# Sixteen tiles of U of layer 1 split into high and low parts beside the mixers, and the layer change's squares summed on TensorE alone

## The chip, the cores and the metric

The kernel runs on one core of a Trainium2 chip. The metric is the device time of one execution in microseconds (us). TensorE (PE) does the matmuls and loads their weights (PEld), VectorE (DVE) and ScalarE (ACT) work element by element, GpSimd (POOL) can do the same, SyncE (SP) issues most of the DMAs, and POOL issues some.

## The reference

A two-layer diffusion backbone over 256 latent and 256 context tokens of width 1024, all in float32:

```python
for l in range(DEPTH):                                  # DEPTH = 2
    n = modulate(rmsnorm(h, norm1_g[l]), shift, scale)
    p = split(n @ w_in[l])                              # inputs of four mixers and the gates
    ys = [neighborhood_attention, hyena, gqa, diff_attention]   # each on its part of p
    h = h + mod * merge_branches(ys, gates, w_branch[l], w_out[l])
    m = modulate(rmsnorm(h, norm2_g[l]), shift, scale)
    h = h + mod * peer(m, peer_wq[l], peer_keys[l], peer_u[l], peer_v[l])
    # layer 1: latent tokens alone
return rmsnorm(h_lat, final_g)

def peer(x, wq, keys, u_tab, v_tab):    # 16384 experts, 8 heads, top 16 of each
    q = x @ wq;  s = q . keys           # two lists of 128 scores for each head
    best, eidx = top16 of the sums of the two top-16 lists
    g = softmax(best)
    return sum over the chosen experts e: g[e] * gelu(u_tab[e] . x) * v_tab[e]
```

## The kernel before

**Products in float32.** A weight tile `r` (128x1024 float32, 512 KB) is split into a high part `wh` (a rounded copy, made by ACT) and a low part `wl = r - wh` (a subtract on DVE or POOL). `mm3` makes each product of three matmuls (L405 to L407: hi with hi, lo with hi, hi with lo). The raw tiles, the high parts and the low parts each rotate through three buffers (`wraw`, `wh`, `wl`), and all users of weights share these nine.

**Units.** The projections, the gates, the output projection and the query projection come as a list of units (`unit_order`) in each layer: six of neighbourhood attention (`na`), four of `gqa`, six of differential attention (`dif`), 32 gates with six of Hyena (`hyn`) ahead of the ninth, then `out` and `wq`. `Units.load` issues a unit's DMA on SP (L313), `Units.split` makes its two parts (L336 on ACT, L337 on DVE or POOL), `Units.next` splits one or two units ahead and loads up to three ahead. An entry `pre` in this list is a tile of U: it is loaded and split in the same way, and its low part is stored to DRAM by SP (L339, `ulo`). In layer 0 there are 20 of them among the mixers' units; in layer 1 there are none.

**PEER.** Instead of fetching the chosen experts, the kernel computes all 128 tiles of U against the tokens (`u_next`: `load_u` on SP, `split_u` at L1247 and L1248, `u_mm` into `po`, Gelu into a `ga` buffer), scatters the gates g into a dense table of 128x128 per token (`scatter`: one-hot rows `ohA`, `ohB`, `ohC` on DVE and ACT, matmuls at L1560, copies `gblk` at L1562, stores to `gd`), and then multiplies the gated activations with the 128 tiles of V (L1698). The search for the best experts is `lists` (MAX8, MATCH_REPLACE8, FIND_INDEX8 at L1383 to L1387) and `select` (L1442 to L1488), on DVE. U tiles are woven between these as work for PE. For a tile that was a `pre`, `load_u` fetches the low part from DRAM by a DMA on POOL's queue (L1244) and no subtract is made. In layer 1 (256 tokens, so a U tile is 24 matmuls of 128x256) the first 15 low parts are made by POOL and those after them by DVE.

**The change of layers.** After the last tiles of V, the sums are transposed on PE (L401), added to the state `hT` on DVE (L1801), and the next layer's norm is begun: `Rms` squares each 128x256 piece on ACT (L456), adds the squares in pairs on DVE (L462), and sums over the partitions by a matmul with ones (L463); `rstd_of` (L411 to L415) gives the factor, and `norm_apply` (L484 to L486) the normed `nh` and `nl`. At this place alone the squares lie in quarters of tiles of the `wl` and `wh` rings (`Rms(..., "wl")` for tokens 256 to 511, `Rms(0, 256, ew, "wh")` for tokens 0 to 255); other norms use small buffers of their own.

The order of the instructions on each engine is that in which a scheduler put them when the kernel was built; within an engine they start in that order.

Of the kernel before, what the change touches and what calls it, by code (L numbers as in the profile page):

```python
# [8 lines left out]
F32 = mybir.dt.float32  # L9
# [10 lines left out]
P = 128  # L20
D = 1024
KD = 8
T = 512
EPS = 1e-6
DEPTH = 2
# [38 lines left out]

N_PRE = (20, 0)


def unit_order():  # L70

    o = []
    for l in range(DEPTH):
        pre = iter(range(N_PRE[l]))
        proj = lambda kind, n: [x for i in range(n) for x in [(l, 'pre', j) for j in ([] if kind == 'na' and i == 0 else
                                                                                       [next(pre, None)]) if j is not None] + [(l, kind, i)]]
        o += proj('na', 6)
        o += proj('gqa', 4)
        o += proj('dif', 6)
        for i in range(32):  # L80
            if i == 8:
                o += proj('hyn', 6)
            o += [(l, 'gate', i)]
            if N_MOD1 + i < (N_MOD2 if l else N_MOD):
                o += [(l, 'modr', N_MOD1 + i)]

        for kind in ('out', 'wq'):
            o += [(l, kind, i) for i in range(8)] * (1 if l else 2)
        o += LATE_MOD[l]
    return o  # L90
# [58 lines left out]
def lay_out(i):  # L149
# [21 lines left out]
    for l in range(DEPTH):  # L171
# [14 lines left out]
        for k, w in parts.items():  # L186
            for m, u in enumerate(w):
# [18 lines left out]
                                 g['diff_lq2'][l], g['diff_lk2'][l]]))  # L206
        HB.append(g['hy_bias'][l][None])
    order = unit_order()
    a['W'] = np.stack([U[k] for k in dict.fromkeys(order) if k[1] != 'pre'])
    a['WB'] = np.stack(WB)  # L210
# [63 lines left out]
def body(ctx, tc, I, out, dbg=None):  # L274
    nc = tc.nc
    pe, act, dve, pool, sp = nc.tensor, nc.scalar, nc.vector, nc.gpsimd, nc.sync
# [5 lines left out]
    dr = ctx.enter_context(tc.tile_pool(name="dr", bufs=1, space=DRAM))  # L282
# [13 lines left out]
    def po_tile():  # L296
        tick[0] ^= 1
        return psp.tile([P, 512], F32, name=f"po{tick[0]}")

    order = unit_order()  # L300
    place = {k: z for z, k in enumerate(k for k in dict.fromkeys(order) if k[1] != 'pre')}
    ulo_d = [[dr.tile([P, D], F32, name=f"ulo{l}_{j}") for j in range(N_PRE[l])] for l in range(DEPTH)]

    class Units:
        def __init__(self):
# [60 lines left out]
    start = stx.enter_context(tc.tile_pool(name="start", bufs=1))  # L366
# [19 lines left out]
    ones = keep.tile([P, P], F32, name="ones")  # L386
# [52 lines left out]
    class Rms:  # L439
# [17 lines left out]

        def sum(self, k):

            if k % 2:  # L460
                a, b = [self.sq.pop(z)[:, :self.n] for z in (k - 1, k)]
                dve.tensor_tensor(a, a, b, op=ALU.add)  # L462
                pe.matmul(self.ps[:, :self.n], ones, a, start=(k == 1), stop=(k == KD - 1))  # L463
# [122 lines left out]
    for l in range(DEPTH):  # L586
        last = l == DEPTH - 1
        q0 = 256 if last else 0
        n = T - q0
# [648 lines left out]
        def load_u(j):  # L1238
            if j < P:
                ur[j] = wp.tile([P, D], F32, name="wraw", bufs=3)  # L1240
                sp.dma_start(ur[j], I['U'][l, j])
                if j < N_PRE[l]:
                    ul[j] = wp.tile([P, D], F32R, name="wl", bufs=3)
                    pool.dma_start(ul[j], ulo_d[l][j])  # L1244

        def halves(h, lo, r, eng=dve):
            act.activation(h, r, AF.Copy)  # L1247
            return eng.tensor_tensor(lo, r, h.bitcast(F32), op=ALU.subtract)  # L1248

        def split_u(j):  # L1250
            if j >= P:
                return
            h = wp.tile([P, D], F32R, name="wh", bufs=3)
            if j < N_PRE[l]:
                lo = ul.pop(j)
                act.activation(h, ur.pop(j), AF.Copy)
            else:
                lo = wp.tile([P, D], F32R, name="wl", bufs=3)
                halves(h, lo, ur.pop(j), lo_eng[0])
            us[j] = (h, lo)  # L1260
# [23 lines left out]
        def u_next():  # L1284
            j = nu[0]
            if j == 0:
                load_u(0)
                load_u(1)
                split_u(0)
            load_u(j + 2)  # L1290
            split_u(j + 1)
            u_mm(j)
            nu[0] += 1
# [558 lines left out]
```

## Time and profile before

| | before |
|---|---|
| runs | 3037.76, 3040.68, 3041.22 us (median 3040.68) |
| profiled execution | 3041.57 us, its span 3039.8 us |
| busy over the span | PE 2935.4 us, DVE 2270.2, ACT 1480.8, POOL 531.3 |
| granted TensorE clock, mean | 0.989 of full speed |
| layer 1: change of layers / mixers / routing with the first U tiles | 1838 to 1880 / 1880 to 2170 / 2200 to 2350 us |

The span starts with the first instruction on the core and ends with the last; 1.77 us of the profiled execution lie outside it. Busy times of engines overlap. PE is busy nearly all the time, so what counts is how long PE stands still at each place and what it stood waiting for, and, where matmuls are queued but start late, how far their spacing is above the densest one.

### The profile page before, as it was taken

Reading aid. Unit: us, or ns where it says so; the run is one execution under the profiler, and the core shown is the slowest. Engines: PE = TensorE matmul, PEld = TensorE weight load, DVE = VectorE, ACT = ScalarE, POOL = GpSimd, SP = SyncE. Lnnn points to the kernel's source line nnn. Section 1 sums busy time; section 2 is a strip of 40 time slices with the busy share of each in tenths; the row PEclk is TensorE's granted clock in tenths of the full one; section 3 lists DMA queues with packets and bytes.
Section 4 is the critical chain, followed back from the end, with each engine's and each line's share of the span. In section 5 each row is a group of like instructions: output and inputs, shape, how many; then the busy total and the mean of one; then the engine's idle time right before and its main releaser. Section 6 shows DMA issues by size and latency. Waiting matters only on the chain.

```text
span 3039.8 us, 47523 instructions
## 1 busy us (share of the span) xinstructions
PE 2935.4 (97%) x17500; PEld 2593.4 (85%) x17500; DVE 2270.2 (75%) x4818; ACT 1480.8 (49%) x2603; POOL 531.3 (17%) x394
## 2 busy tenths in 40 slices
PE   8999999998999999999999998999899999999998
PEld 5877777897889999999999986888898989989986
DVE  5875986799888777777877687788699667555545
ACT  5555422559853333333333335565548754555443
POOL 1001110140023444444444102000160000000000
PEclk9999999999999999999999999999999999999999
DMA  8544344655689998998988764357555699666644
GB/s 309 180 142 139 119 151 142 200 189 195 230 296 344 326 323 305 312 330 315 321 320 314 266 194 138 96 182 226 193 160 202 214 300 316 217 208 208 211 150 146
DMA packets 271673, 693.42 MB, mean 228 GB/s; under 512 B 22440, under 2 KB 115120, under 8 KB 270928
## 3 DMA queue, kind: packets, MB, share of 16 engines
q1 hardware_dynamic: 228096, 534.85, 52.6%
q0 software_dynamic: 43344, 155.54, 14.7%
q8 instruction: 137, 2.24, 0.3%
q14 instruction: 96, 0.79, 0.1%
HBM read 630.53 MB, written 59.77 MB: 227 GB/s over the span
## 4 chain that ended last, share of the span: by engine, by line
PE 73%; DVE 11%; DMA 4%; ACT 2%; issue 2%; POOL 0%; DVEq 0%; ACTq 0%; POOLq 0%; SPq 0%
PE mm L1698 13%; PE at L1698 12%; PE po L405 9%; PE po L407 9%; PE po L406 9%; PE mm L405 5%; PE mm L406 5%; PE mm L407 5%; PE at L1560 3%; DMA vr<-in_V_dram 2%; DMA wraw<-in_W_dram 2%; PE at L401 1%; DVE junk L527 1%; ACT vh L1247 1%; DVE rep L1385 1%
## 5 line engine op out<-in xcount | busy, mean ns | idle before, releaser
L405 PE MATMUL po<-nh,wh 128*128 128x384 f32 (+1 forms) x2048 | 636.7, 311 | 4.9 <-ACT wh L1247 2.2
L407 PE MATMUL po<-nh,wl 128*128 128x384 f32 (+1 forms) x2048 | 633.9, 310 | 3.2 <-DVE wl L1248 2.6
L1247 ACT ACTIVATE wh<-wraw 128x1024 fp32r<-128x1024 f32 x236 | 249.8, 1059 | 363.5 <-PE po L406 324.0
L405 PEld LDWEIGHTS po<-nh,wh 128*128 128x128 f32 x2048 | 389.3, 190 | 14.5 <-ACT wh L1247 2.8
L407 PEld LDWEIGHTS po<-nh,wl 128*128 128x128 f32 x2048 | 388.8, 190 | 4.9 <-DVE wl L1248 3.5
L1248 DVE TENSOR_TENSOR vl<-vr,vh 128x1024 fp32r<-128x1024 f32 x254 | 310.5, 1222 | 108.4 <-ACT vh L1247 108.1
L1247 ACT ACTIVATE vh<-vr 128x1024 fp32r<-128x1024 f32 x254 | 269.7, 1062 | 232.0 <-DMA vr<-in_V_dram 201.9
L405 PE MATMUL mm<-nh,wh 128*128 128x256 f32 (+1 forms) x1056 | 349.2, 333 | 13.6 <-ACT wh L336 4.2
L1248 DVE TENSOR_TENSOR wl<-wraw,wh 128x1024 fp32r<-128x1024 f32 x221 | 269.6, 1221 | 117.8 <-ACT wh L1247 117.7
L407 PE MATMUL mm<-nh,wl 128*128 128x256 f32 (+1 forms) x1056 | 343.3, 326 | 0.4 <-POOL wl L337 0.4
L406 PE MATMUL po<-nl,wh 128*128 128x384 f32 x1024 | 343.7, 336 | 0.0
L336 ACT ACTIVATE wh<-wraw 128x1024 fp32r<-128x1024 f32 x176 | 185.5, 1057 | 293.5 <-PE mm L406 162.4
L406 PE MATMUL mm<-nl,wh 128*128 128x256 f32 (+1 forms) x992 | 325.1, 329 | 0.0
L406 PE MATMUL po<-nh,wh 128*128 128x256 f32 x1024 | 289.8, 283 | 0.0
L1698 PE MATMUL mm<-vl,Wh 128*128 128x512 f32 x635 | 250.3, 394 | 4.3 <-DVE vl L1248 4.0
L1698 PE MATMUL mm<-vh,Wh 128*128 128x512 f32 x635 | 248.4, 391 | 0.9 <-ACT vh L1247 0.8
L1698 PE MATMUL at<-vh,Wl 128*128 128x512 f32 x635 | 248.5, 391 | 0.0
L1698 PE MATMUL at<-vh,Wh 128*128 128x512 f32 x635 | 248.2, 391 | 0.0
L1698 PE MATMUL mm<-vh,Wl 128*128 128x512 f32 x635 | 247.4, 390 | 0.0
L1698 PE MATMUL at<-vl,Wh 128*128 128x512 f32 x635 | 247.0, 389 | 0.0
L405 PEld LDWEIGHTS mm<-nh,wh 128*128 128x128 f32 x1056 | 205.0, 195 | 40.4 <-ACT wh L336 4.6
L1332 DVE SCALAR_TENSOR_TENSOR gacc<-grow,gdot,gacc 128x1024 f32<-128x1024 f32 x127 | 162.9, 1283 | 90.6 <-DMA grow<-in_V_dram,gix 89.6
(369 smaller groups left out, 6288.2 us busy)
## 6 DMA issues: line engine op xcount, KB each, us to landing
wraw<-in_U_dram SPq DMA_DIRECT2D x276, 512.0 KB
vr<-in_V_dram SPq DMA_DIRECT2D x254, 512.0 KB
wraw<-in_W_dram SPq DMA_DIRECT2D x214, 512.0 KB
gd<-gblk SPq DMA_DIRECT2D x80, 512.0 KB
G<-gd SPq DMA_DIRECT2D x32, 768.0 KB
G<-gd SPq DMA_DIRECT2D x32, 512.0 KB
grow<-in_W_dram SPq DMA_DIRECT2D x24, 512.0 KB
ulo<-wl SPq DMA_DIRECT2D x20, 512.0 KB
```

Source lines behind the costliest of these rows:

```text
L336: act.activation(h, r, AF.Copy)
L401: pe.transpose(o, i, ident)
L405: pe.matmul(ps, w[0], x[0], start=first, stop=False)
L406: pe.matmul(ps, w[0], x[1], start=False, stop=False)
L407: pe.matmul(ps, w[1], x[0], start=False, stop=last)
L527: dve.scalar_tensor_tensor(w if s else junk, w, 1.0, crow[s], op0=ALU.mult, op1=ALU.mult, accum_out=mod[:, u, s:s + 1])
L1247: act.activation(h, r, AF.Copy)
L1248: return eng.tensor_tensor(lo, r, h.bitcast(F32), op=ALU.subtract)
L1332: dve.scalar_tensor_tensor(acc, g, dot[:, e:e + 1], acc, op0=ALU.mult, op1=ALU.add)
L1385: dve.match_replace(rep[:, :nn], v[:, 0:8], x, -3e38)
L1560: pe.matmul(ps4[:, :, z], A[:, :, z], C[:, z, :, h], start=h == 1, stop=h == 0)
L1698: pe.matmul(accs[i][h], w[a][:, i * 128:(i + 1) * 128], v[b][:, h * 512:(h + 1) * 512], start=j == 0 and a + b == 0, stop=j == P - 1 and a ...
```

## The change

The table of pre-made tiles becomes a range for each layer: 0 to 19 in layer 0 as before, and 14 to 29 in layer 1, one ahead of each of the four `gqa`, six `dif` and six `hyn` units of layer 1. Second, where an `Rms` keeps its squares in a ring, the pairwise adds are left out and each of the eight squares goes through its own matmul with ones. Lines from 462 on move down by two.

```diff
-N_PRE = (20, 0)
+PRE = (range(20), range(14, 30))
...
-        pre = iter(range(N_PRE[l]))
-        proj = lambda kind, n: [x for i in range(n) for x in [(l, 'pre', j) for j in ([] if kind == 'na' and i == 0 else
+        pre = iter(PRE[l])
+        proj = lambda kind, n: [x for i in range(n) for x in [(l, 'pre', j) for j in ([] if kind == 'na' and (i == 0 or l) else
...
-    ulo_d = [[dr.tile([P, D], F32, name=f"ulo{l}_{j}") for j in range(N_PRE[l])] for l in range(DEPTH)]
+    ulo_d = [[dr.tile([P, D], F32, name=f"ulo{l}_{j}") for j in range(PRE[l].stop)] for l in range(DEPTH)]
...
         def sum(self, k):
 
-            if k % 2:
+            if self.ring is not None:
+                pe.matmul(self.ps[:, :self.n], ones, self.sq.pop(k), start=(k == 0), stop=(k == KD - 1))
+            elif k % 2:
                 a, b = [self.sq.pop(z)[:, :self.n] for z in (k - 1, k)]
                 dve.tensor_tensor(a, a, b, op=ALU.add)
                 pe.matmul(self.ps[:, :self.n], ones, a, start=(k == 1), stop=(k == KD - 1))
...
-                if j < N_PRE[l]:
+                if j in PRE[l]:
                     ul[j] = wp.tile([P, D], F32R, name="wl", bufs=3)
                     pool.dma_start(ul[j], ulo_d[l][j])
...
-            if j < N_PRE[l]:
+            if j in PRE[l]:
                 lo = ul.pop(j)
                 act.activation(h, ur.pop(j), AF.Copy)
```

The change of layers, DVE's order before, from the first residuals (`hT`) to the first normed piece (`n_x`):

```order
L1801 SCALAR_TENSOR_TENSOR hT<-at,mod_113,hT 128x256 x3
L462 TENSOR_TENSOR wl<-wl 128x256
L1801 SCALAR_TENSOR_TENSOR hT<-mm,mod_113,hT 128x128
L462 TENSOR_TENSOR wl<-wl 128x256
L1801 SCALAR_TENSOR_TENSOR hT<-mm,mod_113,hT 128x128 x7
L412 TENSOR_SCALAR n_t<-po_17404 128x256
L462 TENSOR_TENSOR wh<-wh 128x256
L413 TENSOR_TENSOR n_t<-n_t,n_r_17493 128x256
...
L415 SCALAR_TENSOR_TENSOR n_r_17493<-n_t,n_r_17493 128x256
L462 TENSOR_TENSOR wh<-wh 128x256
L484 SCALAR_TENSOR_TENSOR n_x<-hT,coef_116,n_r_17493 128x256 x3
```

The same place on PE now, from the transposes of the sums of V (`at`, `mm`) to the first projection (L405); L461 is the matmul with ones:

```order
L401 MATMUL at<-kc,grow 128x128 x4
L401 MATMUL mm<-kc,grow 128x128 x3
L401 MATMUL at<-kc,grow 128x128 x4
L461 MATMUL po_17434<-wl,ones 128x256 x4
L401 MATMUL at<-kc,grow 128x128 x6
L401 MATMUL mm<-kc,grow 128x128 x2
...
L461 MATMUL po_17434<-wl,ones 128x256 x3
L401 MATMUL mm<-kc,grow 128x128 x2
L461 MATMUL po_17520<-wh,ones 128x256 x7
L649 MATMUL at<-k_17641,k_17639 64x256
L405 MATMUL mm<-nh,wh 128x256 x2
```

The adds of L462 are gone from DVE, sixteen sums stand on PE where eight stood, four of them between the transposes, and seven in one row right ahead of the projection.

SP's order in the mixers of layer 1, where before there was one load after another of units (L313, with L316 for the gates' second weight):

```order
L316 DMA wbraw<-in_WB_dram 128x256 x3
L313 DMA wraw<-in_W_dram 128x1024 x18
L316 DMA wbraw<-in_WB_dram 128x256
```

and now, from the first gqa unit on:

```order
L313 DMA wraw<-in_U_dram 128x1024
L316 DMA wbraw<-in_WB_dram 128x256
L339 DMA ulo_14_103<-wl 128x1024
L313 DMA wraw<-in_W_dram 128x1024
L313 DMA wraw<-in_U_dram 128x1024
L339 DMA ulo_15_104<-wl 128x1024
L313 DMA wraw<-in_W_dram 128x1024
```

Each store of a low part stands ahead of the loads of the next unit and the next tile of U, and those are issued only after it.

POOL's order in the routing of layer 1, where before fifteen subtracts stood in one row:

```order
L1248 TENSOR_TENSOR wl<-wraw,wh 128x1024 x15
```

and now, with the loads of the low parts of tiles 14 to 29 (L1246):

```order
L1250 TENSOR_TENSOR wl<-wraw,wh 128x1024 x13
L1246 DMA wl<-ulo_14_103 128x1024
L1250 TENSOR_TENSOR wl<-wraw,wh 128x1024
L1246 DMA wl<-ulo_15_104 128x1024
L1246 DMA wl<-ulo_16_105 128x1024
```

One subtract of POOL is gone and sixteen DMAs are there. On DVE the subtracts of tiles 15 to 29, which stood among the searches and one-hot rows, are gone from this stretch:

```order
L1522 TENSOR_TENSOR ohA<-iota_21657,iT 128x1024
L1248 TENSOR_TENSOR wl<-wraw,wh 128x1024 x2
L1385 MATCH_REPLACE rep<-sv,mm 128x128
L1538 TENSOR_TENSOR ohC<-ohB,gT 128x512
L1386 MAX sv<-rep 128x8
```

That was one such place of before; now the first of DVE's subtracts in layer 1 stands behind both searches.

## Rows read from the trace of the kernel before

**Rows 1.** The page, part 1: busy time, share of the span, instructions.

```profile
PE 2935.4 (97%) x17500; PEld 2593.4 (85%) x17500; DVE 2270.2 (75%) x4818; ACT 1480.8 (49%) x2603; POOL 531.3 (17%) x394
```

**Rows 2.** PE's waits, 2240 to 2350: total us, times, longest us.

```profile
PE po L407 <- DVE wl L1248: 2.6, 4, 0.9
PE po L405 <- ACT wh L1247: 2.2, 2, 1.4
PE at L1560 <- ACT gblk L1562: 1.5, 3, 0.7
```

**Rows 3.** Groups by line, 2264 to 2350: busy us, mean ns | idle before.

```profile
L405 PE MATMUL po<-nh,wh 128*128 128x256 f32 x119 | 34.9, 294 | 2.2 <-ACT wh L1247 2.2
L1560 PE MATMUL at<-ohC,ohA 128*128 128x128 f16 x256 | 32.2, 309 | 1.8 <-ACT gblk L1562 1.5 <-DVE ohA L1522 0.3
...
L1418 PE MATMUL mm<-keys,hT 64*128 64x128 f32 x32 | 4.6, 285 | 0.0
...
L1248 DVE TENSOR_TENSOR wl<-wraw,wh 128x1024 fp32r<-128x1024 f32 x14 | 16.8, 1214 | 3.0 <-ACT wh L1247 3.0
```

**Rows 4.** Busy by stretch (PE, PEld, DVE, ACT, POOL, clock, DMA, GB/s); sum 2264:2350.

```profile
2280.00:2290.00 10.00, 10.00 (x85) 9.21 (x84) 10.00 (x40) 9.89 (x30) 0.00 (x0) 1.00 0.01 2
...
2340.00:2350.00 10.00, 7.80 (x62) 7.25 (x62) 6.89 (x12) 5.50 (x9) 0.00 (x0) 1.00 0.73 291
sum 86.00, PE 79.50 PEld 75.11 DVE 82.52 ACT 71.51 POOL 3.54; mean PE 9.94 PEld 9.39 DVE 10.31 ACT 8.94 POOL 0.44
```

**Rows 5.** The chain of waits, 2335 to 2350.

```profile
2338.34 7.95 DMA wraw<-in_U_dram
```

**Rows 6.** PE's waits in layer 0's routing, 650 to 830.

```profile
PE at L1560 <- ACT gblk L1562: 11.2, 17, 1.4
...
PE po L407 <- DMA wl<-ulo: 0.5, 1, 0.5
```

**Rows 7.** Busy time by stretch in layer 0's routing.

```profile
660.00:670.00 10.00, 10.00 (x59) 10.00 (x59) 9.76 (x61) 6.35 (x8) 1.06 (x2) 1.00 0.92 321
...
740.00:750.00 10.00, 10.00 (x60) 9.84 (x59) 10.00 (x53) 8.24 (x22) 1.06 (x2) 1.00 1.00 355
```

**Rows 8.** Instructions on `ulo`: min/median/max ns, first and last start.

```profile
L339 SPq DMA_DIRECT2D ulo<-wl x20: 326/327/330, 37.7 to 303.8; - x20
L1244 POOL DMA_DIRECT2D wl<-ulo x20: 530/530/570, 653.7 to 820.7; - x20
```

**Rows 9.** Busy time by stretch in the mixers of layer 1.

```profile
1910.00:1940.00 30.00, 27.13 (x188) 23.79 (x187) 28.45 (x129) 12.09 (x31) 2.44 (x4) 0.94 0.29 80
...
2020.00:2040.00 20.00, 20.00 (x162) 18.45 (x161) 18.46 (x39) 11.31 (x21) 0.00 (x0) 1.00 0.30 94
2040.00:2120.00 80.00, 74.58 (x580) 70.19 (x580) 73.83 (x189) 41.90 (x76) 0.00 (x0) 1.00 0.69 218
```

**Rows 10.** PE's waits in these mixers, and line 337 there.

```profile
PE at L401 <- DVE k L1100: 2.6, 1, 2.6
PE at L401 <- DVE g_t L423: 1.8, 1, 1.8
...
L337 DVE TENSOR_TENSOR wl<-wraw,wh x43: 1205/1220/1227, 1881.2 to 2128.3; 128x1024 fp32r<-128x1024 f32 x43
```

**Rows 11.** Timelines of PE, DVE, POOL, change of layers: start us, us.

```profile
1846.17 2.04 PE L463 MATMUL po<-wh,ones 128*128 128x256 f32 x6 [1.42 <-DVE wh L462]
1852.47 1.22 PE L463 MATMUL po<-wh,ones 128*128 128x256 f32 x2 [4.27 <-DVE wh L462]
1853.41 0.80 PE L405 MATMUL mm<-nh,wh 128*128 128x256 f32 x2
...
1847.37 2.57 DVE L415 SCALAR_TENSOR_TENSOR n_r<-n_t,n_r 128x256 f32<-128x256 f32 x1
1849.86 2.56 DVE L462 TENSOR_TENSOR wh<-wh 128x256 f32<-128x256 f32 x1
...
1847.27 4.86 POOL L337 TENSOR_TENSOR wl<-wraw,wh 128x1024 fp32r<-128x1024 f32 x2 [6.41 <-ACT wh L336]
```

## The prediction

> **What bounds the kernel now.** I read the page first: PE is busy for 97% of the span, the others for much less [rows 1], so only the places where PE stands still or spaces its matmuls out can be won. Three of them are touched: the routing of layer 1 with its U tiles, the mixers of layer 1, and the change of layers.
>
> In the routing, PE's waits name the low part (DVE, 2.6 us), the high part (2.2 us) and the scatter's copies on ACT (1.5 us) [rows 2]. By stretches, PE stands idle 86.00 - 79.50 = 6.5 us there, while DVE is busy 82.5 of 86 us and ACT 71.5, with both full from 2280 on [rows 4]. Busy time hides wide spacing, so I count as well: 3 x 119 matmuls of U (L405, L406, L407), 256 of the scatter and 32 of the scores are 645 in 86 us [rows 3]; the fully busy stretch has 85 in 10 us, of the same mixture [rows 4], so 645 would take 75.9 us. What PE loses is 86 - 75.9 = 10.1 us. That is all there is to win in the routing.
>
> In the mixers PE loses little: 30 - 27.13 = 2.9 us in 1910 to 1940 and 80 - 74.58 = 5.4 in 2040 to 2120 [rows 9], mostly for DVE [rows 10]. There DVE is nearly full: 28.45 of 30 us, 18.46 of 20, 73.83 of 80 [rows 9]. At the change of layers PE waits 1.42 and 4.27 us for DVE's adds [rows 11]: while POOL made two subtracts (4.86 us), the DVE instructions L415 and L462 took 2.57 and 2.56 us.
>
> **The routing's relief.** Removed are 15 subtracts of DVE (tiles 15 to 29), of 1.214 us; 14 of them lie in this stretch, 16.8 us [rows 3], and DVE falls from 82.5 to about 66 of 86 us. One subtract of POOL goes too, which PE does not wait for. ACT's copies stay, all of them. The gain lies between nothing, if ACT holds PE as long as DVE did, and 10.1 us. Layer 0's routing shows what is left when low parts come from DRAM: 0.5 us of waits for them, but 11.2 us for the scatter's copies on ACT in 180 us [rows 6]. In 86 us that rate makes 5.3 us, which I expect to stay. The gain is then 10.1 - 5.3 = 4.8; I take **-5 us**.
>
> **The sixteen loads.** Each costs POOL 0.53 us of issue [rows 8]; POOL's subtracts are nearly over by then, and they are hidden. Their bytes are not so surely hidden: in the new order 264 matmuls of U, 11 tiles, stand in one run between the two scatters, at 24 x 10/85 = 2.8 us a tile [rows 4], and each tile now brings two times 0.524 MB, 374 GB/s. Layer 0 moved 355 GB/s with PE fully busy, and 321 in another stretch with PE busy too [rows 7]. At 355 a tile takes 2.95 us, at 321 3.27: 11 x 0.13 = 1.4 to 11 x 0.45 = 5 us more; nothing if the loads spread into the scatters' time, where the queue has room. I take **+1**, since the three buffers let some of them run ahead.
>
> Here the Trainium skill speaks against the change. Row first: in layer 0, 20 such loads were issued by POOL [rows 8] beside a DVE that was busy 9.76 and 10.00 of 10 us [rows 7], and PE waited for one of them, 0.5 us [rows 6]. The Trainium skill, "SBUF — State Buffer", section "SBUF: two separate sides", says that a DMA from the GpSimd queue has its descriptors written by software, which is locked out while DVE runs an instruction that holds both ports; its example goes from about 620 to about 3100 ns. By the row the loads cost nothing beyond their bytes; by that rule each could come some 2.5 us later, an estimate from that page, which would not change the sum as long as two tiles of lead cover it, and is a rival below where they don't.
>
> **The mixers' burden.** Added are 16 loads, 16 ACT copies, 16 DVE subtracts of 1.22 us [rows 10], 19.5 us in all, and 16 stores of 0.33 us issue on SP [rows 8]. ACT has room (12.09 of 30, 11.31 of 20, 41.90 of 80 [rows 9]), and so has the DMA (shares 0.29 to 0.69). DVE hasn't everywhere. In the order the subtracts of four of the tiles stand with the units split in 1910 to 1940: 4 x 1.22 = 4.9 us, where DVE has 30 - 28.45 = 1.55 free, 3.3 over. Three of the Hyena stage stand in 2020 to 2040: 3.7 us against 1.54 free, 2.1 over, with only 6.2 us of room in the 80 us after. The other nine lie where DVE has slack. What is behind a subtract on DVE is attention and normalisation that PE waits for [rows 10]. So 5.4 us are late, and not all reach PE, since its queue has other units: I take **+3.5**, between 0 (PE's order covers it) and 12 (the ring, below).
>
> **The change of layers.** Eight adds leave DVE, one of which POOL held for 2.56 us. Eight matmuls with ones come to PE: six records, three sums, take 2.04 us [rows 11], so 8 x 0.68 = 5.4 us. PE's idle time ahead of the first projection is 1.42 + 4.27 = 5.7 us, and PE's new order has all sixteen sums but no gap between them and the projection, so PE gets there at best 5.7 - 5.4 = 0.3 us earlier. On the other path, the factor of the first half now waits for four sums that stand ahead of the later transposes, about 4 x 0.68 = 2.7 us; against this the four adds of `wh` that stood among L412 to L415 and ahead of L484 are gone, 2.56 us for the last and 3 x 0.33 before. L413 to L415 will still meet POOL's two subtracts. Bounds: -3 (the normed pieces come earlier by all the adds) and +2 (the sums hold back transposes and residuals, and nothing is regained); I take **-1**.
>
> **Sum.** -5 + 1 + 3.5 - 1 = -1.5 on the profiled execution's 3041.57, that is 3040.1; this execution lies 0.9 above the median, so **3039.2** on the median's scale of 3040.68. About 0.2%, 6 us, is what a measurement of this kernel tells from no change; the forecast is no change, with its own range 3035 to 3046.
>
> **The rivals.**
> *The routing's loss goes in full* (faster). DVE's 16.8 us were also what made ACT's one-hot rows and copies late; ACT was idle 14.5 of 86 us [rows 4]. For it: DVE is the only engine that is full over the whole stretch. Against: layer 0's 11.2 us. -10 + 0 + 1 - 1 = -10: 3030.7.
>
> *The change does nothing there* because ACT takes DVE's place as the bound from 2280 to 2330, and the late wait behind a raw tile's transfer, 7.95 us [rows 5], stays: 0 + 1 + 3.5 - 1 = +3.5, 3044.2, still within 0.2%.
>
> *The ring stalls the mixers* (slower). A low part's buffer is one of three and is given back only when its store has landed, and SP issues the next loads behind that store. It is held for 1.22 + 0.33 us and the store's landing, at least 0.524 MB at 355 GB/s, 1.5 us, and at most the 7.95 us of the longest transfer named: 3.0 to 9.5 us. The next unit but one, whose split needs the buffer, is due after two units of PE, 5.6 us. So PE can be 3.9 us late in a place where units stand close together; three such places make 12. Instead of 3.5 that gives 3047.7. For it: DVE's full stretches; against: 20 stores in layer 0 had the same ring, though units there are longer. It decides from 11 us of burden in the mixers on.
>
> *The loads of low parts come late in the run of 11 tiles* (slower). If each took 7.95 us [rows 5], with two tiles of lead, a tile would take 3.98 in place of 2.8 us: 11 x 1.18 = 13 us in place of 1, 3051. It decides from a landing time of 5.6 us. That is where the skill's rule above would lead; layer 0 speaks against it.
>
> **How the numbers follow.** Forecast 0.33; routing in full 0.28; nothing in the routing 0.16; ring 0.17; late loads 0.06. Faster by over 0.2%: 0.30 (the first rival and the lower edge of the forecast); same 0.47; slower 0.23. The range reaches down past the full relief (3030.7), and up past the ring (3047.7), leaving out the late loads and the edges: 3029 to 3049.
>
> **What would show it.** In the routing, DVE should be clearly below full between 2290 and 2340, the wait of L407 for the low part should be gone, and waits for `gblk` should stay or grow; PE's idle time should fall from 6.5 to about 3 us. In the mixers, waits of PE on DVE near 1920, 2060 and 2090 should be longer by 3 to 4 us in all; more than 11, with waits on L337's low parts, would be the ring. At the change of layers the waits on L462 should be gone, PE full with sums from 1844 to 1852, and the first projection within 1 us of where it was. The prediction is wrong if the subtracts on DVE cost PE nothing in the mixers, or if ACT follows DVE's relief and the routing gets dense, or if the sums on PE, by leaving it no gap, change more than the 0.3 us that I gave them.

## The result and the profile after

The changed kernel took 3064.11 us (median of four runs, 3059.55 to 3071.39) against 3040.69 of the kernel before: 1.0075 times, 95% interval 1.0058 to 1.0091. It is slower by 23 us, where no change was forecast. The profiled execution took 3061.99 us, its span is 3059.6.

The page, part 1, of the kernel after, beside [rows 1]:

```profile
PE 2940.5 (96%) x17516; PEld 2596.0 (85%) x17516; DVE 2268.2 (74%) x4811; ACT 1493.5 (49%) x2619; POOL 536.6 (18%) x409
```

PE has only the 16 records of the added sums more, and stands still longer. To see where, I set the starts of the same matmuls side by side: the n-th projection matmul, the n-th matmul of U and of V. Each column is one profiled execution minus that of before, in us.

| place (time in before) | after | e1 | e9 | e11 | e6 | e5 | e4 | e16 |
|---|---|---|---|---|---|---|---|---|
| first projection of layer 1 (1853) | -3.9 | -3.3 | -1.7 | -1.3 | +0.4 | +0.6 | -1.4 | -6.5 |
| na units done (1880) | +2.2 | +1.4 | +5.6 | +4.1 | +5.2 | +3.5 | +2.1 | -0.2 |
| gqa, dif (1958) | +12.9 | +0.8 | +6.0 | +13.9 | +7.2 | +10.0 | +12.8 | +3.0 |
| ahead of the Hyena units (2004) | +13.4 | +0.8 | +6.0 | +13.9 | +8.7 | +11.7 | +14.6 | +3.4 |
| in the Hyena units (2022) | +20.3 | +0.8 | +6.0 | +13.9 | +14.1 | +11.6 | +20.4 | +3.6 |
| mixers done (2165) | +24.3 | +2.2 | +8.5 | +16.4 | +15.7 | +17.7 | +23.0 | +2.1 |
| first tile of U (2224) | +22.8 | +0.8 | +9.6 | +17.6 | +14.9 | +17.4 | +22.0 | +3.1 |
| routing done (2363) | +19.6 | +2.4 | +7.5 | +15.9 | +13.5 | +15.3 | +19.3 | +2.4 |
| first tiles of V (2483) | +22.4 | +1.9 | +10.5 | +18.3 | +17.2 | +19.2 | +23.2 | +4.0 |

How far two executions can differ shows in runs that are the same there. As built, e9 is instruction by instruction the program of e3, and e12 that of e5; the mixers of e1 hold the same instructions in the same order as those of e3. From 1880 to 2165 e1 loses 0.8 us, e3 7.3 and e9 2.9, and e5 and e12 lose 14.2 and 13.9. So over the whole of the mixers a few us say nothing. The executions of e9 and e11 are the longest of their kernels, 5.8 and 5.4 us above the medians.

The mixers of layer 1, from 1880 to 2165, lose 24.3 - 2.2 = 22.1 us (22.2 in e2, the tiles alone). The routing gains 22.8 - 19.6 = 3.2, and the first tiles of V give back 2.8.

**The mixers.** Busy time by stretch, after, where [rows 9] stood before (PE, PEld, DVE, ACT, POOL, clock, DMA share, GB/s):

```profile
1910.00:1940.00 30.00, 23.75 (x156) 20.36 (x157) 27.27 (x109) 16.34 (x30) 2.44 (x4) 0.94 0.71 218
1940.00:1960.00 20.00, 15.42 (x85) 11.35 (x83) 15.41 (x53) 9.38 (x24) 0.00 (x0) 0.83 0.18 54
...
2030.00:2040.00 10.00, 5.92 (x20) 2.76 (x20) 3.72 (x5) 5.62 (x10) 0.00 (x0) 0.66 0.71 254
```

DVE is not fuller than before (27.27 of 30 us, before 28.45), and in the last row, where PE stands still for 4 us, DVE is idle for 6.3 us. PE's largest waits from 1884 to 1975 and from 2015 to 2060, beside [rows 10]:

```profile
PE mm L401 <- DVE k L800: 8.0, 3, 4.6
```

```profile
PE at L405 <- ACT k L964: 4.1, 1, 4.1
```

What PE waits for is attention: the rotation of its operands on DVE (L800), and the copy of the transposed exponentials on ACT (L964). For weights it waits 3.1 us in all the mixers. The chain of waits of after, 2022 to 2037, says why ACT's copy is late:

```profile
2024.34 1.23 DVE wl L337
...
2025.59 7.69 DMA wraw<-in_U_dram
...
2033.36 1.06 ACT wh L336
2034.42 0.49 ACT k L964
...
2034.95 0.79 PE at L405
```

A subtract on DVE frees a raw buffer; only then SP's load of the next tile of U can start; it takes 7.69 us; ACT, which does its work in order, stands before the copy of that tile, and the exponentials that PE needs are behind that copy. PE waits 4.1 us, and by the end of the wait the granted clock has fallen to 0.50 of full speed, its lower level (1.2 GHz, not 2.4):

```profile
2036.00:2038.00 2.00, 2.00 (x11) 1.14 (x12) 1.29 (x2) 1.77 (x3) 0.00 (x0) 0.50 0.03 10
```

```profile
2036.10 3.67 PE L1041 MATMUL po<-k,v 128*64 128x256 f32 x14
```

The next matmuls are slow as well: fourteen of L1041 take 3.67 us, where the last fourteen of the same sixteen took 1.95 in before.

The largest of the waits for L800, 4.6 us up to 1946.5, has another chain:

```profile
1919.57 4.16 DMA ulo<-wl
1923.85 1.22 DVE wl L337
...
1933.41 1.14 DVE wl L337
1936.16 1.14 DVE wl L337
...
1941.57 1.23 DVE wl L337
...
1946.50 0.45 PE mm L401
```

Here a subtract waits until a store of a low part has landed (4.16 us), and behind it DVE works with hardly a gap, with subtracts between the small instructions of attention. So this wait is for DVE's queue, with the subtracts in it.

SP's own waits in after, 1885 to 2060, and its issues around 1915:

```profile
SPq L339 <- DVE wl L337: 45.2, 6, 21.1
SPq L313 <- DVE wl L337: 35.8, 14, 5.5
```

```profile
1914.67 0.33 SPq L339 DMA_DIRECT2D ulo<-wl  x1
1915.09 0.38 SPq L313 DMA_DIRECT2D wraw<-in_W_dram  x1
1916.12 0.33 SPq L313 DMA_DIRECT2D wraw<-in_U_dram  x1
1919.57 0.33 SPq L339 DMA_DIRECT2D ulo<-wl  x1
1919.98 0.64 SPq L313 DMA_DIRECT2D wraw<-in_W_dram  x1
```

In these two cases the load of a unit's weights goes out 0.4 us behind the store, that is, as soon as the store that stands ahead of it has got its subtract.

**The routing.** Busy time by stretch in after, the same columns, beside [rows 4]; the sum is over 2286 to 2372:

```profile
2302.00:2312.00 10.00, 10.00 (x87) 8.99 (x86) 10.00 (x42) 9.92 (x30) 0.53 (x1) 1.00 0.18 54
2312.00:2322.00 10.00, 10.00 (x89) 9.71 (x87) 10.00 (x45) 10.00 (x30) 0.53 (x1) 1.00 0.73 265
2322.00:2332.00 10.00, 8.55 (x72) 7.73 (x71) 9.92 (x44) 10.00 (x27) 0.53 (x1) 1.00 0.78 279
2332.00:2342.00 10.00, 10.00 (x88) 9.61 (x86) 9.90 (x64) 10.00 (x30) 1.05 (x2) 1.00 0.66 222
2342.00:2352.00 10.00, 10.00 (x87) 9.77 (x86) 9.52 (x27) 9.95 (x27) 1.06 (x2) 1.00 0.99 350
2352.00:2362.00 10.00, 8.79 (x75) 8.55 (x73) 2.43 (x7) 7.04 (x10) 1.06 (x2) 1.00 1.00 362
2362.00:2372.00 10.00, 8.14 (x64) 7.53 (x63) 0.15 (x1) 4.22 (x7) 1.05 (x2) 1.00 1.09 406
sum 86.00, PE 81.47 PEld 77.31 DVE 65.59 ACT 70.65 POOL 9.65; mean PE 10.18 PEld 9.66 DVE 8.20 ACT 8.83 POOL 1.21
```

DVE fell from 82.5 to 65.6 us, as worked out (66); ACT stayed at 70.65 (before 71.51) and is full from 2302 to 2352; PE's idle time fell from 6.5 to 4.5 us. From 2352 on the DMA is full (362 and 406 GB/s) and PE loses 3 us there, 1.7 of them for a load of a low part.

**The start of V.** PE's timeline in after:

```profile
2466.86 0.50 PE L1700 MATMUL mm<-vh,Wh 128*128 128x512 f32 x1 [1.11 <-ACT vh L1249]
...
2477.00 0.50 PE L1700 MATMUL mm<-vh,Wh 128*128 128x512 f32 x1 [1.15 <-ACT vh L1249]
```

The kernel before has no such wait there. The chain of after puts the first of them behind V's transfer:

```profile
2460.15 5.51 DMA vr<-in_V_dram
2465.75 1.06 ACT vh L1249
```

**The change of layers**, PE's timeline in after, beside [rows 11]:

```profile
1842.48 3.19 PE L461 MATMUL po<-wh,ones 128*128 128x256 f32 x14
1849.48 0.79 PE L405 MATMUL mm<-nh,wh 128*128 128x256 f32 x2 [3.23 <-ACT nh L487]
...
1865.01 0.80 PE L407 MATMUL mm<-nh,wl 128*128 128x512 f32 x1 [4.79 <-DVE wl L337]
```

The 14 records of the sums take 3.19 us, 0.46 a sum and not 0.68. The first projection starts 3.9 us earlier than before, and then PE waits 4.79 us for a unit's low part, a wait that before had not.

### The profile page after: what moved, and what is told of

Its sections match the earlier page's. It is cut to its first block, busy times and chain, and to the rows that moved or that the text cites. A ratio compares the mean times of both kernels' runs of the same rounds, so it can differ in the third digit from the quotient of the medians.

```text
span 3059.6 us, 47656 instructions
## 1 busy us (share of the span) xinstructions
PE 2940.5 (96%) x17516; PEld 2596.0 (85%) x17516; DVE 2268.2 (74%) x4811; ACT 1493.5 (49%) x2619; POOL 536.6 (18%) x409
## 4 chain that ended last, share of the span: by engine, by line
PE 66%; DVE 10%; DMA 8%; issue 5%; ACT 3%; POOL 1%; DVEq 0%; ACTq 0%; SPq 0%; POOLq 0%
PE mm L1700 12%; PE at L1700 11%; PE po L405 8%; PE po L407 8%; PE po L406 8%; PE mm L405 4%; PE mm L407 4%; PE mm L406 4%; PE at L1562 3%; DMA wraw<-in_W_dram 3%; DMA vr<-in_V_dram 2%; DVE wl L337 1%; DMA grow<-in_UR_dram,gix 1%; ACT vh L1249 1%; DVE junk L529 1%
## 5 line engine op out<-in xcount | busy, mean ns | idle before, releaser
L405 PE MATMUL po<-nh,wh 128*128 128x384 f32 (+1 forms) x2048 | 636.7, 311 | 2.8 <-ACT wh L1258 1.5
L405 PEld LDWEIGHTS po<-nh,wh 128*128 128x128 f32 x2048 | 389.2, 190 | 12.5 <-ACT wh L1258 2.5
L405 PE MATMUL mm<-nh,wh 128*128 128x256 f32 (+1 forms) x1056 | 348.9, 332 | 14.6 <-ACT wh L336 4.7
L1250 DVE TENSOR_TENSOR wl<-wraw,wh 128x1024 fp32r<-128x1024 f32 x206 | 251.7, 1222 | 133.5 <-ACT wh L1249 133.3
L405 PEld LDWEIGHTS mm<-nh,wh 128*128 128x128 f32 x1056 | 204.6, 195 | 40.3 <-issue 5.7
L337 DVE TENSOR_TENSOR wl<-wraw,wh 128x1024 fp32r<-128x1024 f32 x153 | 186.5, 1220 | 68.7 <-ACT wh L336 54.6
```

Source lines behind the costliest of these rows:

```text
L337: (pool if order[m][1] == 'wq' or order[m][:2] == (1, 'na') and order[m][2] < 2 or order[m][0] == 0 and order[m][1] in ('gate', 'hyn') and ...
L405: pe.matmul(ps, w[0], x[0], start=first, stop=False)
```

## The experiments

Ratios are to the kernel before on the same chip, with 95% intervals; 0.001 is 3.0 us. Two theories stood at first for the mixers: D, that the subtracts' time on DVE is the cost, and Q, that the stores are (SP's queue, and low parts held until they have landed).

**e1, the sums alone** (before, with the edit of `Rms.sum`).

> The kernel before with the second edit alone: the layer change's sixteen squares each through its own matmul, no tile of U moved. In the trace of the changed kernel the first projection came 1.6 us earlier, but the stretch from 1853 to 1880, where PE then waits 4.8 us for the low part of a projection unit, came out 6.1 us longer. Theory S (the sums put the low part's subtract later on DVE): this kernel shows that wait too and is 3 to 6 us above before, about 3045. Theory P (the pre-made tiles' loads put it late): this kernel has no such wait and lies 1 to 4 us below before, about 3038.

Measured 3044.99 us, 1.0010 (0.9999 to 1.0022). (In after the first projection came 3.9 us earlier, as in the table, not 1.6.) The same wait is there, so the sums make it (theory S):

```profile
PE mm L407 <- DVE wl L337: 4.8, 1, 4.8
```

The size is at the low end, about 3 us by the medians, and the interval reaches no change.

**e2, the tiles alone** (after, with the pairwise adds back).

> The kernel before with the first edit alone: 16 tiles of U split beside the mixers of layer 1, the squares still added in pairs. If the mixers' burden is the cause of all of the loss, the mixers of layer 1 are about 22 us longer than before and the routing about 3 us shorter: 3059 to 3064. If the sums cause part of it by the order that they leave behind, this kernel lies 4 us or more below the changed kernel.

Measured 3064.29 us, 1.0073 (1.0048 to 1.0098). The tiles make the loss by themselves; the intervals are too wide to see the sums' 3 us in the difference.

**e3, the routing's relief alone.**

```diff
-                    pool.dma_start(ul[j], ulo_d[l][j])
+                    pool.dma_start(ul[j], ulo_d[l][j] if l == 0 else I['U'][l, j])
-        pre = iter(PRE[l])
+        pre = iter(PRE[l] if l == 0 else ())
```

> The changed kernel without the tiles of U in the mixers of layer 1: nothing is loaded, split or stored there, and the routing's loads fetch the raw tile of U in place of its low part (so the products of these 16 tiles are not the reference's). The bytes and queues of the routing are those of the changed kernel. It gives the relief by itself. If the mixers lose 22 us and nothing else, it is 3037 to 3040; if the loads in the routing cost what the subtracts did, it is 3041 or more; a relief of 5 us or more, as forecast, would show as 3036 or less.

Measured 3045.38 us, 1.0015 (1.0001 to 1.0028), no faster than e1: the relief as a whole is worth nothing that can be measured, though the intervals would hide some 3 us. The traces say the same: in all thirteen runs with the sixteen loads in the routing, the stretch from 2224 to 2363 gains 1.4 to 3.5 us, and the stretch from there to the first tiles of V loses 2.4 to 3.9 (e1, without them: 1.6 lost, 0.5 gained).

**e4, no stores** (the `pre` entries as in after, the routing's loads as in e3).

```diff
-                    sp.dma_start(ulo_d[order[m][0]][order[m][2]], lo.bitcast(F32))
+                    if order[m][0] == 0: sp.dma_start(ulo_d[order[m][0]][order[m][2]], lo.bitcast(F32))
```

> The changed kernel with its 16 loads, copies and subtracts in the mixers, but without the 16 stores of low parts (the routing's loads fetch the raw tile of U instead, so those products are not the reference's). A low part's buffer is free at the subtract's end, and nothing stands ahead of the next loads on SP. Theory Q (stores: SP's queue and the ring of three): the mixers' loss falls from 22 us to 6 or less, the time to 3042 to 3047. Theory D (VectorE's time for the subtracts, 19.5 us in nearly full stretches): the loss stays above 15 us, 3055 or more.

Measured 3060.13 us, 1.0055 (1.0038 to 1.0073): theory Q falls as the main cause. By the ratios the stores are worth some 6 us of 23, but the interval overlaps that of after, and in the traces the mixers lose 20.9 us against 22.1.

**e5, no stores and no loads** of U in the mixers (copy and subtract of a part of `hT` that is unused there).

```diff
+                if order[m][:2] == (1, 'pre'):
+                    self.raw[m] = hT[:, 4:, :256]
+                    self.loaded += 1
+                    continue
...
```

> As e4 (no stores), and the 16 loads of U in the mixers left out too: each copy and subtract reads a quarter of the state's buffer that is unused there, so no raw tile of the ring is taken and no transfer is waited for (the split parts are thrown away, and the routing fetches raw tiles as in e4). Theory R (raw tiles: a ring of three and a load that starts only when a subtract has freed a buffer, with ScalarE's copy and what stands behind it waiting for it): the mixers lose 7 us or less, the time is 3043 to 3050. Theory D (VectorE's 19.5 us of subtracts): it stays where e4 was, 3056 or more.

Measured 3060.67 us, 1.0062 (1.0045 to 1.0080). By time that is theory D; but in the trace the step in the Hyena units (+6.9 after, +5.8 in e4) is gone (-0.1), as R says of that place, and other steps come later. All the traces agree on that step. From 2004 to 2022 it is 5.4 to 8.7 us in the runs that load sixteen tiles of U beside the mixers (after, e2, e4, e6, e7, e15; in e8 1.8, and 11.1 more up to 2040), and at most 0.2 in all the others, e16 with its eight tiles among them.

**e6, no stores and no subtracts** (e4 with load and copy alone).

```diff
+                lo = None if order[m][:2] == (1, 'pre') else wp.tile([P, D], F32R, name="wl", bufs=3)
+                if order[m][:2] != (1, 'pre'): (pool if ... else dve).tensor_tensor(lo, r, ...)
```

> As e4 (no stores), and the 16 subtracts left out: load of the raw tile and ScalarE's copy alone (the low part of these tiles is not made). Theory D: 3043 to 3050, since VectorE has no more work than before. Theory R: the raw tile is freed by the copy instead of the subtract, a few us sooner, so 3052 or more.

Measured 3059.24 us, 1.0051 (1.0033 to 1.0069). With no subtract at all more than half of the loss stays: 1.0051 is 0.0036 above e3, after 0.0060; in the traces the mixers lose 10.5 us against 22.1. So D is not needed for that part. Now the Hyena step is there (+5.4) and that in gqa and dif is small (+2.0). Ahead of the Hyena units, from 1880 to 2004, the runs with the sixteen subtracts on DVE (after, e2, e4, e5, e11, e12) lose 8.2 to 12.5 us, e6 3.5, and e1, e3 and e9 from -0.6 to 4.8. That would be DVE's share of the loss; but e10, which has no subtract either, loses 8.5 there, so it isn't shown.

**e7, raw tiles in a buffer of their own** (e5's place in `hT`, with load, subtract and store). **e8**, the same with the stores on POOL's queue (`pool.dma_start`).

```diff
+                if order[m][:2] == (1, 'pre'):
+                    self.raw[m] = hT[:, 4:, :256]
+                    sp.dma_start(self.raw[m], I['U'][1, order[m][2]].rearrange("p (a b) -> p a b", b=256))
...
```

> The changed kernel complete, with the 16 raw tiles of U loaded into an unused quarter of the state's buffer instead of the ring of three; stores and subtracts as in the changed kernel. Theory R: the units' raw tiles come as early as before, and the time falls to 3050 or less. Theory Q (stores on SP's queue and low parts held until they land): little changes, 3058 or more. Theory D the same, 3058 or more.

> As e7, with the stores of low parts issued by POOL, which has no other work there, so that nothing waits on SP for a subtract. If R and Q together are the cause, it is at 3046 or less and tells whether the tiles can be made beside the mixers for nothing; if VectorE's time is the cause it stays above 3056. The relief in the routing is the same as in the changed kernel, and e3 came out no faster than before, so I expect none of these to beat the kernel before.

Measured 3071.84 us, 1.0096 (1.0080 to 1.0113), and 3090.66 us, 1.0166 (1.0134 to 1.0199). Both are slower than after, which no theory said. The one buffer brought a wait of its own: SP holds the next tile's load, and the units' loads behind it, until the tile before has landed and been split. In e8 the new load's waits on SP are these (L314 is the load into `hT`):

```profile
SPq L314 <- DMA hT<-in_U_dram: 32.1, 10, 4.4
SPq L314 <- DVE wl L344: 31.2, 2, 20.4
```

So they do not tell R, Q and D apart; they show a queue that stops, in kernels that are slower than after.

**e9, the entries alone** (e5 with nothing made for an entry), **e10**, with the 16 copies, **e11**, with copies and subtracts outside the rings:

```diff
                 r = self.raw.pop(m)
+                if order[m][:2] == (1, 'pre'):
+                    act.activation(r, r, AF.Copy)                       # e11
+                    dve.tensor_tensor(r, r, r, op=ALU.subtract)         # e11
+                    continue
```

> As e5, with the 16 entries for tiles of U still in the list of units of layer 1 but nothing made for them: no load, no copy, no subtract, no buffer. What stays is the list itself: a unit is split and loaded a fixed number of entries ahead, so each unit's load is now issued about one unit ahead instead of two. Theory A (the shortened lead of the units' loads and splits): 3054 or more. Theory E (the engines' queues and buffers taken by the copies and subtracts): as e3, 3042 to 3048.

> As e9, with ScalarE's 16 copies back, each into a buffer of the ring of high parts (17 us of ScalarE in 280 us in which it is busy half of the time; the source lies in the state's unused quarter, nothing else is made). Theory A: as e9. Theory H (a tile's high part takes one of three buffers, so ScalarE's copy waits for TensorE to be done with an earlier unit, and ScalarE's other work stands behind it): 3052 or more, and clearly above e9.

> As e9, with ScalarE's 16 copies and VectorE's 16 subtracts of a 128x1024 tile, but in the state's unused quarter alone (the subtract is of the copy from itself): the engines' time is spent, no ring is touched, nothing is loaded or stored. Theory D (VectorE's time): 3052 or more. Theory H or A: within 3 us of e9.

Measured 3044.53 us, 1.0011 (1.0002 to 1.0021); 3046.06 us, 1.0014 (1.0005 to 1.0024); 3052.02 us, 1.0038 (1.0024 to 1.0052). The built program of e9 is that of e3: entries for which nothing is made leave no trace in the order into which the scheduler puts the instructions. So e9 measures e3 a second time, no shorter lead was made, and theory A is not tested. The copies in the ring of high parts cost at most some 3 us beside it (H falls). In e11 the copies and subtracts cost 0.0038 - 0.0011, some 8 us; but no ring paces them there, and all sixteen subtracts run within 65 us, where those of e5 are spread over 161. The rows of e11 and of e5:

```profile
L340 DVE TENSOR_TENSOR hT<-hT x16: 1202/1216/1225, 1871.6 to 1936.5; 128x1024 f32<-128x1024 f32 x16
```

```profile
L343 DVE TENSOR_TENSOR wl<-hT,wh x16: 1206/1218/1227, 1888.4 to 2049.2; 128x1024 fp32r<-128x1024 f32 x16
```

So the 8 us are the price of the engines' time in that placement, not in after's.

**e12, e5 with the units' loads two entries further ahead.**

```diff
-                self.load(self.n + 3)
+                self.load(self.n + 3 + (2 if order[self.n + 1][:2] == (1, 'pre') else 0))
```

> As e5 (copies and subtracts in the rings, no load and no store of U), with the units' loads issued two entries further ahead, which is as many units ahead as before the change. Theory A: it comes down from e5's 3060.7 to 3050 or less. Any other theory: within 4 us of e5.

Measured 3054.68 us, 1.0050 (1.0033 to 1.0067), 6 us below e5 by the medians and 4 by the ratios. But the built program is that of e5, instruction by instruction: a load that stands earlier in the source is not issued earlier, since the scheduler sets the order. So e12 is a second measurement of e5, its distance from e5 is noise, and theory A stays untested.

**e13 and e14, the sums for one half of the tokens.**

```diff
-            if self.ring is not None:
+            if self.ring == 'wh':           # e14: 'wl'
```

> The kernel before with the second edit for the squares of tokens 0 to 255 alone (the wh tiles), whose adds stood ahead of the normed pieces; the other half's adds stay. e1 showed 3.6 us more with both halves, with the first projection 3 us earlier and then a wait of 4.8 us for a unit's low part. If the wait came from PE's four sums between the transposes (the wl half), this kernel has the gain without it: 3036 to 3040. If it comes from leaving out the wh half's adds, it is as e1, 3043 to 3047.

> The counterpart of e13: the second edit for tokens 256 to 511 alone (the wl tiles). If the wl half holds back the transposes and residuals, 3043 to 3047 here and no loss in e13; if the wh half is the cause, 3039 to 3043 here.

Measured 3044.16 us, 1.0019 (1.0006 to 1.0033), and 3050.65 us, 1.0036 (1.0023 to 1.0048). By the medians the half of the `wl` tiles, whose sums stand between the transposes, costs the more, but the intervals overlap; e14 lies above both of its forecasts, e13 is no gain either, and both halves together (e1) cost less than the one. Neither of the two traces has the wait of 4.8 us for a low part, so it takes both halves to make it. Which wait makes the rest isn't settled.

**e15, subtracts and stores of the 16 tiles on POOL.**

```diff
-                (pool if order[m][1] == 'wq' or ...
+                (pool if order[m][1] == 'wq' or order[m][:2] == (1, 'pre') or ...
-                    sp.dma_start(ulo_d[order[m][0]][order[m][2]], lo.bitcast(F32))
+                    (pool if order[m][0] else sp).dma_start(ulo_d[order[m][0]][order[m][2]], lo.bitcast(F32))
```

> The changed kernel with the 16 subtracts in the mixers made by POOL (2.4 us each, POOL is idle there) and the stores issued by POOL right behind them, so that neither SP nor VectorE waits or works for them; loads, copies and rings as in the changed kernel. If VectorE's time and SP's queue are two thirds of the burden, as e11 (7.5 us over e9) and e4 (4 us) say, it is 3050 or less. If the rings and the raw tiles' loads are enough by themselves, as e6 (no subtract, no store, 3059) says, it stays at 3057 or more.

Measured 3088.45 us, 1.0154 (1.0128 to 1.0181): much worse, not better. SP now waits for POOL,

```profile
SPq L313 <- POOL wl L337: 83.6, 16, 9.4
```

and still waits 76.4 us for DVE's other subtracts. A subtract of POOL takes 2.37 us (median of 16) where DVE's took 1.22, so it holds the raw buffer longer; that this makes the whole of the loss is not shown.

**e16, eight tiles in place of 16.**

```diff
-PRE = (range(20), range(14, 30))
+PRE = (range(20), range(22, 30))
-        ... ([] if kind == 'na' and (i == 0 or l) else
+        ... ([] if kind == 'na' and (i == 0 or l) or l and i % 2 == 0 else
```

> The changed kernel with 8 tiles of U (22 to 29) in the mixers in place of 16, one ahead of every second unit. If each tile costs its share, the loss over e3 is half of the changed kernel's 19 us: 3053 to 3056. If the loss comes from two entries for each unit in three buffers, which then is nearly gone, 3046 to 3050.

Measured 3046.70 us, 1.0020 (1.0007 to 1.0032). Half of the tiles cost not half of the loss but nearly nothing beside e1 and e3: the mixers' step is 2.1 + 0.2 = 2.3 us in its trace. Only this choice of eight was run: that it is their number, and not the places of the other eight, is not shown. PE's largest waits for DVE in the mixers are now these (3.6 us for L800, where after had 8.0; the second is that of [rows 10]):

```profile
PE mm L401 <- DVE k L800: 3.6, 2, 3.2
PE at L401 <- DVE g_t L423: 1.8, 1, 1.8
```

## Why the prediction was wrong

**The step that failed is "The mixers' burden", +3.5 with a bound of 12.** It measured 22. The sum was made as room on DVE: 19.5 us of subtracts against idle time, stretch by stretch. That part too was priced low: the engines' time without rings or transfers cost some 8 us in e11, bunched as it was there, where I had 5.4 as late and 3.5 as reaching PE. What I priced only as a rival, and as three places of at most 3.9 us, is the rest, by these ratios some 10 of 18 us: a second entry for each unit goes through three raw, three high and three low buffers, so a unit's tile is loaded when the tile of U before it has been split, and the tile of U when a unit has been. Shown are the two ends of it: more than half of the loss is there without subtracts (e6), without loads (e5) and without stores (e4), and it is nearly gone with one tile for every second unit (e16). The chain at 2024 to 2035 shows one case from end to end, and its step goes with the loads in all the runs; the chain up to 1946 shows the subtracts themselves and a store in PE's way. Whether the parts add up is open. Above e3, after loses 18 us, e4 12, e5 14 and e6 11, and so it seems that the stalls stand in for each other, one showing when another is taken away; but in the traces the mixers of e6 and e5 lose 10.5 and 14.2 us and those of e4, which has the work of both, 20.9, and with e1 and e3 at 0.8 and 7.3 that is nearly a sum. How the rest divides between raw buffers, low buffers and SP's queue in the full kernel stays open as well, since e7, e8 and e15, which were to part them, each brought a new wait.

Of the sufferers I had named one: attention and normalisation behind a subtract on DVE. That PE's "queue has other units" helps where weights are late, and PE waited only 3.1 us for weights. What I did not see is that ACT and DVE stop before a copy or a subtract whose tile is not there yet, and that attention stands behind it. "ACT has room" was true by busy time and irrelevant: an engine with room that works in order still stands before its next instruction. The ring rival's counter-argument, that layer 0 had the same ring, was the part of it that misled: its units multiply up to 512 tokens where layer 1 has 256, so PE has up to twice the work to cover a tile; e16, with two units to a tile, fits that.

**The routing's relief, -5, and the loads, +1**: together -4, measured -3.2 up to the end of the routing. DVE's fall came as said. That the size came out too is in part luck: I had left 5.3 us of waits for the scatter's copies on ACT, at layer 0's rate, and they are 1.5 us, as before, though ACT is full; and that DVE and ACT were both full before held from 2280 to 2330 alone (ACT 7.74 and 5.50 of 10 us after that). What PE lost instead lies behind 2352. The waits for the low part did not vanish: in after, 2246 to 2450, one wait for a load is left,

```profile
PE po L407 <- DMA wl<-ulo: 1.7, 1, 1.7
```

What I missed is what is late next. The 8 MB of low parts pass the DMA ahead of V's first tiles, and V's start comes 2.8 us later for a wait on V's transfer; e1, without these loads, has no such wait, and e3, with them and without the mixers' tiles, has it (2.0 us). e3 says the same in time: nothing is left of the relief. The Trainium skill's rule on loads issued by GpSimd ("SBUF — State Buffer", "SBUF: two separate sides") did not decide here: five such loads were issued from 2302 to 2342, with DVE busy 9.9 of 10 us and more, and PE waited for none of them; the 1.7 us came at 2365, with DVE nearly idle. That rule is on instructions that hold both ports, and whether DVE's in that stretch do, no run shows.

**The change of layers, -1**: the first projection came 3.9 us earlier in after (3.3 in e1; I had 0.3), since a sum took 0.46 us in one row, and POOL's two subtracts, beside which L413 and L414 on DVE took 1.72 and 2.45 us, began at 1842.77 in place of 1847.27. It was given back at once by the wait for a low part, and e1 is 3 us slower by the medians. By that the term was mis-sized by 4 us and had the wrong sign, but e1's interval reaches no change. That it is the new order and not the tiles is shown by e1; why DVE's subtract stands so late in it is not.

**The rivals.** The ring had the right sign, 0.17 of the chance, and half the size. It was priced by the store's landing, and e4, which has no stores, keeps two thirds of the loss, the Hyena step among it. Of the two chains shown, one has a stall by a store's landing (4.16 us, priced as 1.5 to 7.95) and one by the load of a raw tile (7.69 us), which the rival did not have. The forecast and its range had no case above 3051.

## What to carry to other kernels

When work is slipped into a stream that runs through a few shared buffers, count how many entries pass for each unit of the bound engine's work, and not only the room on each engine: here one extra tile for two units was nearly free and one for each unit cost some 18 us. Work that is added in front of something on an in-order engine costs what its latest operand costs everything behind it. And when a stage is relieved by moving bytes to it, look at the next stage's first transfers before booking the gain.

## What was not expected of the hardware

Beside POOL's subtracts in e15 single small DVE instructions with two operands in SBUF became much slower. One of the 24 of L423 took 2297 ns, where their median is 160; one of the eight of L794 took 2444 ns, where the others took 292 to 427. Each started 0.1 us after a POOL subtract (2.36 and 2.37 us) and ended just after it; the other instructions of these two lines took what they took in before. The rows of e15, and its timeline beside the second:

```profile
L423 DVE TENSOR_TENSOR g_t<-g_r 128x4 f32<-128x4 f32 (+1 forms) x24 | 5.8, 247 | 0.3
L794 DVE TENSOR_TENSOR k<-k,cst 128x256 f32<-128x256 f32 (+1 forms) x8 | 5.3, 657 | 3.0 <-ACT k L864 2.9
```

```profile
1949.51 2.44 DVE L794 TENSOR_TENSOR k<-k,cst 128x128 f32<-128x128 f32 x1
...
1949.43 2.37 POOL L337 TENSOR_TENSOR wl<-wraw,wh 128x1024 fp32r<-128x1024 f32 x1 [2.50 <-issue]
```

It is what [rows 11] showed at the change of layers (2.57 us for L415). The Trainium skill, "SBUF — State Buffer", section "Who interferes with whom", has the two engines share one port pair as an exclusive lock; these rows agree with it: the DVE instruction waits until the POOL subtract is over. So a mean over a line hides it, and a few instructions carry all of it.
